# Hybrid decoder trunk: the order of the mixing stage, attention's scores one block ahead, and an output projection in one pass

## The chip, the cores and the metric

The kernel runs on one core of a Trainium2 chip. A core has a matrix engine (TensorE, in the profile PE, with its weight loads as PEld), a vector engine (DVE), a scalar engine (ACT), GpSimd (POOL), SyncE (SP, which here only issues DMAs), and 16 DMA engines. Each engine works through its own instructions in order; they wait for one another by semaphores. The metric is the device time of one execution in microseconds, lower is better.

## What is computed

Two layers over 512 tokens of width 1024, all in float32. Each layer is: half a SwiGLU feed-forward step, a mixing step, half a feed-forward step, each with a norm whose shift, scale and gate come from a condition `c`. The mixing step projects the normed tokens to 2560 columns, which feed three mechanisms side by side, joins their 1024 results and projects these back:

```python
proj = hn @ w_mix_in[l]
p_att, p_rwkv, p_conv = jnp.split(proj, [ATT_PROJ_WIDTH, ATT_PROJ_WIDTH + RWKV_PROJ_WIDTH], axis=-1)
y_att = sliding_window_sink_attention(p_att, ...)    # 8 query heads, 2 key heads, window 128: 512 columns
y_rwkv = rwkv7_time_mix(p_rwkv, ...)                 # 4 heads of a linear recurrence over time: 256 columns
y_conv = short_conv_mix(p_conv, conv_w[l])           # gated convolution of three taps: 256 columns
mixed = jnp.concatenate([y_att, y_rwkv, y_conv], axis=-1) @ w_mix_out[l]
h = h + (1.0 + gt2) * mixed
```

Attention works on blocks of 128 tokens, each against itself and the block before. The recurrence keeps a 64x64 state per head:

```python
def step(S, inp):
    r_t, w_t, k_t, v_t, kk_t, a_t = inp
    s_kk = jnp.einsum('bhvk,bhk->bhv', S, kk_t)
    S = (S * w_t[:, :, None, :] - s_kk[..., None] * (kk_t * a_t)[:, :, None, :]
         + v_t[..., None] * k_t[:, :, None, :])
    return S, jnp.einsum('bhvk,bhk->bhv', S, r_t)
```

## The kernel before

Everything is held with features on the 128 partitions and the 512 tokens along the free axis. The residual `h` is eight tiles of 128x512. Large products are done in three passes: a float32 operand is split into a rounded high part and the rest (`split`, L100: a cast on ACT, a subtraction on DVE), and high x high, high x low and low x high are summed in PSUM. `mm6` (L94) does one weight row of 128 (index `k`) for one output tile, in six matmuls of 256 columns; `mm3` is the same with three. `load_w` (L261) loads a weight tile of up to 128x8x128 on SP's queue into one of two raw buffers (`wraw`) and splits it into a pair of `wH` and `wL`, of which there are four.

The program is written in Python with generators, and a scheduler orders the instructions of each engine: what is written first has priority, and a later instruction goes ahead only where an earlier one isn't expected to be ready. In a few places (`tc.manual_schedule`, `tc.issue_after`) the written order is kept.

`mix` (L585) is the mixing step. Four routines of it run side by side:

- `products()` (L637): the twenty projection tiles (`projector`, L277, each eight `mm6` into a PSUM bank of tag `mm`), what is done with each tile, and then the output projection. The columns' order is set in `lay_out` (L1317): keys, values and four query tiles; then eight recurrent tiles (`lo`, then `k`, `r`, `v` of chain 0 and of chain 1, then `gd`); then six convolution tiles. The first three tiles of a stage use weights that were loaded in the stage before, share their sweep over `k`, and end together. `shifted` (L632) evacuates a recurrent tile with ACT and then DVE.
- `rwkv(0)` and `rwkv(1)` (L756): two chains of two heads each, in blocks of 64 tokens. A set-up (decays, two reciprocals, products of 64-row tiles), the inverse of small triangular matrices (`elim`/`inv` on DVE, with a way through DRAM there and back: `dl`, `G`, `di`, `C`), two levels of products, and at the end six steps of the state one after another (`ps_s`, L977, then DVE into `St`, L978). PSUM tags `r0` and `r1`, SBUF buffers of tags `s0` and `s1` (eight each), `u0`, `u1`.
- `attention()` (L1005): per block `scores(b)` (products `ps_sc`, then the softmax on DVE and ACT in place in `Sc`, L1037), `turned` (transposes `ps_pt` and masks), the product with the values `ps_av`. PSUM tag `x`. `Sc` has two buffers of its own, both of which one block uses.

The driving loop (L1113) lets the live routines take a step in turn. Each step of `rwkv` or `attention` yields its estimated PE time; in proportion to it `products()` is advanced, so that large products stand between the small ones. The proportion is the filling work that is left to the chains' work that is left, from the constants `RWKV_WORK, ATT_WORK, FILL_WORK` (L34); a step of `products()` (one `mm6`) counts 0.65. `attention` starts when the query tiles are there (`done` has "att"), a chain when its three tiles are there.

The output projection has eight output tiles and eight weight rows `k`: rows 0 to 3 multiply attention's results, 4 and 5 the convolution's, 6 and 7 the recurrence's. Output tiles 0 to 5 are done with rows 4, 5, 0, 1, 2, 3 once attention has ended (`done` has "ya") and are added to `h`; tiles 6 and 7 (`last`) are begun in the same way. After the loop, when both chains have ended, rows 6 and 7 are done for tiles 0 to 5 from a weight tensor of their own (`wmo2`, L1120), and these are added to `h` a second time, with the sums of squares for the next norm (`add_ss`). `close` (L382) ends tiles 6 and 7 and does the next norm beside them.

Of the kernel before, what the change touches and what calls it, by code (L numbers as in the profile page):

```python
# [30 lines left out]
PAD = 26  # L31
GAP = 448
GROUPS = ((0, 12), (12, 22))
RWKV_WORK, ATT_WORK, FILL_WORK = 29.8, 15.2, 129.6  # L34


def _columns(spec):
# [20 lines left out]
def trunk_kernel(ctx, tc, ins, out, layers=L, phases=("ffn1", "mix", "ffn2")):  # L58
# [524 lines left out]


    def mix(l, hn, ss, mp, then, ready):  # L585
        wi, wo1, wo2 = ins["wmi"], ins["wmo1"], ins["wmo2"]

        def small(name, w, bufs=2):
            return mp.tile([P, w], F32, name=name, tag=name, bufs=bufs)
# [13 lines left out]
        def EA(name):  # L603
            return mp.tile([P, T], F32, name=name, tag="ea", bufs=3)
# [27 lines left out]
        def shifted(pt, j, z):  # L632

            act(z, pt, AF.Copy, scale=got["om"][:, j : j + 1])
            stt(z[:, 1:], pt[:, : T - 1], mu[:, j : j + 1], z[:, 1:], ALU.mult, ALU.add)
            return z

        def products():
# [16 lines left out]
            ts(a0h, prm(l, "a0"), 0.5, None, ALU.mult)  # L655
            tt(gqk, prm(l, "qg"), prm(l, "kg"), ALU.mult)
            got.update(om=om, w0h=w0h, a0h=a0h)
            sq = EA("ksq")
            act(sq, pt, AF.Square)
            kt = A("kt")  # L660
# [36 lines left out]
            got.update(kt=kt, V=V, qr=qr, rq=rq)  # L697
            done.add("att")

            got["lo"] = shifted((yield from tile_()), 6, S(1, "lo"))  # L700
            act(got["lo"][:64], got["lo"][:64], AF.Tanh)
            for q in range(2):
                k_[q] = shifted((yield from tile_()), 2 + q, S(q, "k"))
                r_[q] = shifted((yield from tile_()), 0 + q, S(q, "r"))
                v_[q] = shifted((yield from tile_()), 4 + q, S(q, "v"))
                done.add(f"rwkv{q}")
            gd = shifted((yield from tile_()), 7, mp.tile([P, T], F32, name="gd", tag="gd"))
            act(gd, gd, AF.Tanh, scale=0.5)
            ts(gd, gd, 0.5, 0.5, ALU.mult, ALU.add)
            got["gd"] = gd  # L710

            yc = []
            for q in range(2):
                pt = yield from tile_()
# [9 lines left out]
                pt = yield from tile_()  # L724
                tt(cv, pt, cv, ALU.mult)
                yc.append(cv)
            xs = [pair(f"y{k}") for k in range(6)]
# [28 lines left out]
        def rwkv(q):  # L756
# [243 lines left out]
            mm(pg, got["gw"][:, cw], got["gd"], start=True, stop=True)  # L1000
            tt(y, y, pg, ALU.mult)
            yr[q] = y
            yield 0.9

        def attention():  # L1005
# [3 lines left out]

            def scores(b):  # L1010
                qs = slice(b * P, (b + 1) * P)
                both = [mp.tile([P, 4, P], F32, name="Sc", tag="Sc", bufs=2) for _ in range(2)]
                if b == 0:
                    for Sc in both:
                        nc.gpsimd.memset(Sc, -1e30)
                for i0 in (0, 2):
                    pts = [psum([P, 2, 2, P], "ps_sc") for _ in range(2)]
                    with tc.manual_schedule(engines={mybir.EngineType.PE}):
                        for i in range(2):
                            for g, pt in enumerate(pts):  # L1020
                                if b:
                                    m = mm(pt[:, i].rearrange("p a c -> p (a c)"), qr[rows[g], i0 + i, qs], kt[rows[g], (b - 1) * P : (b + 1) * P], start=True, stop=True)
                                else:
                                    m = mm(pt[:, i, 1], qr[rows[g], i0 + i, qs], kt[rows[g], qs], start=True, stop=True)
                                behind(m, free[0])
                    for Sc, pt in zip(both, pts):
                        if b:
                            nc.scalar.copy(Sc[:, i0 : i0 + 2], pt[:, :, 0])
                        free[0] = nc.vector.copy_predicated(Sc[:, i0 : i0 + 2], rep("mq", 2).bitcast(I32), pt[:, :, 1])
                    yield 1.0  # L1030
                for g, Sc in enumerate(both):
                    softmax(b, g, Sc)
                return both
# [28 lines left out]
                    both.append((t, src))  # L1062
                return both

            for b in range(NB):
                qs = slice(b * P, (b + 1) * P)
                pm = []
                for Sc in (yield from scores(b)):
                    pm.append(turned(b, Sc))
                    yield 0.4  # L1070
                po = psum([P, 4, P], "ps_av")
                for n in range(len(pm[0])):
                    for g in range(2):
                        t, src = pm[g][n]
                        m = mm(po[rows[g]].rearrange("p i q -> p (i q)"), V[:, src, rows[g]], t, start=n == 0, stop=n == len(pm[0]) - 1)
# [34 lines left out]
                    product_step()  # L1110


        xr = []  # L1113
        for q in range(2):
            x = pair("yr")
            split(*x, yr[q])
            xr.append(x)
# [11 lines left out]
        xs = got["xs"] + xr  # L1129
# [161 lines left out]
def lay_out(i):  # L1291
# [25 lines left out]
    order = [np.r_[512:768], pairs] + [rw(j) for j in (6, 2, 0, 4, 3, 1, 5, 7)]  # L1317
# [6 lines left out]
    w2 = wo[:, 512:768, : 6 * P].reshape(L, 2, P, 2, 3, P)  # L1324
    a["wmo2"] = c(w2.transpose(0, 3, 2, 4, 1, 5).reshape(L, 2, P, 6, P))
    a["lora"] = c(np.concatenate([i["rwkv_w_w2"], i["rwkv_a_w2"]], axis=1))
    a["gw2"] = c(i["rwkv_g_w2"])

# [43 lines left out]
```

## Time and profile before

| | us |
|---|---|
| median of three runs | 1913.11 |
| the three runs | 1912.78, 1913.11, 1916.35 |
| the profiled execution | 1913.21 |
| its span (first to last instruction) | 1911.2 |

A span is shorter than the time of its execution by what lies before the first and behind the last instruction, here 2.0 us. Times in the views count from the span's start. On one core the profiler shows each engine's instructions with their start and duration; who released a waiting engine is inferred from the semaphores. A row of a view of waits has the engine, the waiting tile and line, the engine, tile and line that it waited for, then the total in us, how often, and the longest. Matmuls overlap their neighbours: a matmul of 128x256 lasts 0.28 us by its row, while the next starts 0.114 us later. The two mixings lie at about 382 to 623 us and 1319 to 1561 us of the span.

### The profile page before, as it was taken

The numbers are of one execution on the slowest core, as the hardware profiler recorded it, in microseconds if no ns is written. First come the engines' busy times: TensorE is split into PE (matmuls) and PEld (weight loads), VectorE is DVE, ScalarE is ACT, GpSimd is POOL, SyncE is SP. The second block draws the span as 40 slices with busy tenths as digits, with TensorE's granted clock in tenths as the row PEclk, the third lists the DMA queues.
The fourth block names the chain that finished last, engine by engine and source line by source line (L and its number), as shares of the span: only waits on it lengthen the run. The fifth ranks groups of instructions, "written<-read, shape, count | busy, mean of one in ns | idle before, by whom it ended". The sixth has DMA issues, their size and how long they took to land. (4 is left out here: it accounts for less than half of the span.)

```text
span 1911.2 us, 37042 instructions
## 1 busy us (share of the span) xinstructions
PE 1878.8 (98%) x15504; PEld 1741.7 (91%) x15504; DVE 1399.8 (73%) x2181; ACT 837.0 (44%) x1264; POOL 130.7 (7%) x212
## 2 busy tenths in 40 slices
PE   8999999999999999999999999999999999999999
PEld 7998899897888999899899989989878899988998
DVE  7687687758976877677877776876599667864862
ACT  4443255346322554155345514544562235532551
POOL 0101100100000001110100020010000000110000
PEclk8999999999999999999999999999999999999999
DMA  7767877521312476887727678781321315774741
GB/s 300 245 168 221 271 198 229 168 70 45 79 43 81 123 198 176 278 218 199 264 62 193 171 260 242 191 278 42 93 61 49 88 34 163 209 217 130 198 140 59
DMA packets 104326, 308.46 MB, mean 161 GB/s; under 512 B 23392, under 2 KB 24416, under 8 KB 103136
## 3 DMA queue, kind: packets, MB, share of 16 engines
q1 hardware_dynamic: 75936, 203.33, 32.9%
q0 software_dynamic: 28224, 102.77, 21.7%
q8 instruction: 121, 1.98, 0.4%
q14 instruction: 45, 0.37, 0.1%
HBM read 302.66 MB, written 3.41 MB: 160 GB/s over the span
## 5 line engine op out<-in xcount | busy, mean ns | idle before, releaser
L101 ACT CAST wH<-wraw 128x1024 fp32r<-128x1024 f32 (+2 forms) x292 | 268.4, 922 | 512.6 <-PE ps_mm L91 176.8
L102 DVE TENSOR_TENSOR wL<-wraw,wH 128x1024 fp32r<-128x1024 f32 (+2 forms) x292 | 308.1, 1058 | 96.9 <-ACT wH L101 95.8
L90 PE MATMUL ps_mm<-actH,wH 128*128 128x512 f32 (+1 forms) x784 | 288.5, 368 | 0.0
L91 PE MATMUL ps_mm<-actL,wH 128*128 128x512 f32 (+1 forms) x784 | 288.0, 367 | 0.0
L92 PE MATMUL ps_mm<-actH,wL 128*128 128x512 f32 (+1 forms) x784 | 288.0, 367 | 0.0
L441 PE MATMUL ps_d<-comH,wH 128*128 128x256 f32 x816 | 226.8, 278 | 1.6 <-ACT wH L101 0.8
L443 PE MATMUL ps_d<-comH,wL 128*128 128x256 f32 x816 | 225.8, 277 | 2.3 <-DVE wL L102 2.3
L442 PE MATMUL ps_d<-comL,wH 128*128 128x256 f32 x816 | 225.5, 276 | 0.0
L98 PE MATMUL ps_mm<-hnH,wH 128*128 128x256 f32 x1040 | 214.0, 286 | 5.1 <-ACT hnH L101 2.9
L98 PE MATMUL ps_mm<-hnL,wH 128*128 128x256 f32 x1040 | 211.8, 283 | 0.0
L98 PE MATMUL ps_mm<-hnH,wL 128*128 128x256 f32 x1040 | 209.5, 281 | 0.5 <-DVE wL L102 0.5
L163 DVE SCALAR_TENSOR_TENSOR wada<-wada,crep 128x1024 f32<-128x1024 f32 x140 | 168.0, 1220 | 47.8 <-DMA wada<-in_wadaT 47.6
L102 DVE TENSOR_TENSOR wL<-sum,wH 128x1024 fp32r<-128x1024 f32 x102 | 124.8, 1224 | 74.9 <-ACT wH L101 74.7
L98 PEld LDWEIGHTS ps_mm<-hnH,wH 128*128 128x128 f32 x1040 | 159.5, 190 | 16.1 <-issue 8.2
L92 PEld LDWEIGHTS ps_mm<-actH,wL 128*128 128x128 f32 x784 | 147.8, 189 | 24.4
L90 PEld LDWEIGHTS ps_mm<-actH,wH 128*128 128x128 f32 x784 | 147.8, 189 | 24.2
L91 PEld LDWEIGHTS ps_mm<-actL,wH 128*128 128x128 f32 x784 | 147.8, 189 | 24.1
L101 ACT CAST wH<-sum 128x1024 fp32r<-128x1024 f32 x102 | 107.5, 1054 | 140.3 <-PE ps_d L442 60.1
L98 PEld LDWEIGHTS ps_mm<-hnL,wH 128*128 128x128 f32 x1040 | 160.2, 190 | 6.7 <-issue 5.7
L98 PEld LDWEIGHTS ps_mm<-hnH,wL 128*128 128x128 f32 x1040 | 160.1, 190 | 4.1 <-issue 2.9
L441 PEld LDWEIGHTS ps_d<-comH,wH 128*128 128x128 f32 x816 | 153.2, 188 | 3.9 <-ACT wH L101 1.4
L443 PEld LDWEIGHTS ps_d<-comH,wL 128*128 128x128 f32 x816 | 153.2, 188 | 2.9 <-DVE wL L102 2.9
(402 smaller groups left out, 4237.3 us busy)
## 6 DMA issues: line engine op xcount, KB each, us to landing
wada<-in_wadaT POOLq DMA_DIRECT2D x128, 512.0 KB, 4.9
wraw<-in_wmi SPq DMA_DIRECT2D x40, 512.0 KB
wraw<-in_w2p SPq DMA_DIRECT2D x36, 512.0 KB
wraw<-in_w1p SPq DMA_DIRECT2D x32, 512.0 KB
wraw<-in_w1o SPq DMA_DIRECT2D x32, 384.0 KB
wraw<-in_w2o SPq DMA_DIRECT2D x32, 384.0 KB
wraw<-in_w1i SPq DMA_DIRECT2D x20, 512.0 KB
wraw<-in_w1o SPq DMA_DIRECT2D x32, 320.0 KB
```

Source lines behind the costliest of these rows:

```text
L90: mm(acc, wH, xH, start=start, stop=False)
L91: mm(acc, wH, xL, start=False, stop=False)
L92: mm(acc, wL, xH, start=False, stop=stop)
L98: mm(acc[:, sl], w[a][:, k], x[b][:, sl], start=start and n == 0 and sl is HALVES[0], stop=stop and n == 2, skip_group_check=True)
L101: nc.scalar.copy(hi, src)
L102: nc.vector.tensor_sub(lo, src, hi.bitcast(F32))
L163: stt(w, w, 1.0, crep, ALU.mult, ALU.mult, accum_out=out_)
L441: mm(pt[:, i], wH, x[k][0], start=start and i + k == 0, stop=False, skip_group_check=True)
L442: mm(pt[:, i], wH, x[k][1], start=False, stop=False, skip_group_check=True)
L443: last = mm(pt[:, i], wL, x[k][0], start=False, stop=k == 3, skip_group_check=True)
```

## The change

- The columns of the first projection, and with them the steps of `products()`, come in another order: the eight recurrent tiles first, then keys, values and queries, then the convolution. So chain 0 starts after the fourth tile and chain 1 after the seventh, attention after the fourteenth.
- The squares of the queries (`qsq`) are held in general buffers (tag `e`) and not in those of the chains.
- `attention()` computes the scores and the softmax of block b+1 before the values of block b. `Sc` has no buffers of its own any more; it takes buffers of chain 0 (tag `s0`), four at a time instead of two.
- The output projection takes all eight rows in one pass. `products()` waits for both chains ("y0", "y1"), splits their results, and opens output tiles 0 to 3 with rows 4 to 7, in PSUM tags `r0` and `mm` in turn, with their weight pairs held. When attention has ended, rows 0 to 3 of these follow, then tiles 4 and 5 with all eight rows, then `last` as before. `wmo2`, the pass after the loop and the second addition to `h` are gone; the sums of squares are made with the one addition.
- `FILL_WORK` is 114.4 instead of 129.6.

```diff
-RWKV_WORK, ATT_WORK, FILL_WORK = 29.8, 15.2, 129.6
+RWKV_WORK, ATT_WORK, FILL_WORK = 29.8, 15.2, 114.4
...
             got.update(om=om, w0h=w0h, a0h=a0h)
+            got["lo"] = shifted(pt, 6, S(1, "lo"))
+            act(got["lo"][:64], got["lo"][:64], AF.Tanh)
+            for q in range(2):
+                k_[q] = shifted((yield from tile_()), 2 + q, S(q, "k"))
+                r_[q] = shifted((yield from tile_()), 0 + q, S(q, "r"))
+                v_[q] = shifted((yield from tile_()), 4 + q, S(q, "v"))
+                done.add(f"rwkv{q}")
+            gd = shifted((yield from tile_()), 7, mp.tile([P, T], F32, name="gd", tag="gd"))
...
+            pt = yield from tile_()
             sq = EA("ksq")
...
-                sqs.append(S(i % 2, "qsq"))
+                sqs.append(E("qsq"))
...
-            done.add("in")
+            while not {"y0", "y1"} <= done:
+                yield "stuck"
+            for k in (6, 7):
+                split(*xs[k], yr[k - 6])
+
+            def out(pt, w, ks, first=False, last=False):
+                for k in ks:
+                    mm6(pt, w, k, xs[k], first and k == ks[0], last and k == ks[-1])
+                    yield
+
+            early, late = (4, 5, 6, 7), (0, 1, 2, 3)
+            open_ = []
+            for i in range(4):
+                w, pt = load_w(wo1[l, i]), psmm(("r0", "mm"))
+                yield from out(pt, w, early, first=True)
+                open_.append((i, w, pt))
             while "ya" not in done:
                 yield "stuck"
             for k in range(4):
                 split(*xs[k], qr[:, k])
-
-            got["xs"] = xs
-            for i in range(KD - 2):
-                w = load_w(wo1[l, i, :, :6], 6)
-                pt = psmm()
-                for k in (4, 5, 0, 1, 2, 3):
-                    mm6(pt, w, k, xs[k], k == 4, k == 3)
-                    yield
-                residual(pt, i, cm, None)
+            for i, w, pt in open_:
+                yield from out(pt, w, late, last=True)
+                residual(pt, i, cm, ss)
+            for i in (4, 5):
+                w, pt = load_w(wo1[l, i]), psmm()
+                yield from out(pt, w, early + late, first=True, last=True)
+                residual(pt, i, cm, ss)
...
-                both = [mp.tile([P, 4, P], F32, name="Sc", tag="Sc", bufs=2) for _ in range(2)]
+                both = [S(0, "Sc", (P, 4, P)) for _ in range(2)]
...
+            last = None
+            for b in range(NB):
+                both = yield from scores(b)
+                if last is not None:
+                    yield from values(b - 1, last)
+                last = both
+            yield from values(NB - 1, last)
             done.add("ya")
...
-        for n in range(2):
-            w = load_w(wo2[l, n], 6)
-            for d in range(3):
-                i = 3 * n + d
-                pt = psmm(BANKS[1:3])
-                for k in range(2):
-                    mm6(pt, w, 2 * d + k, xr[k], k == 0, k == 1)
-                residual(pt, i, cm, ss)
             steps[-1](n, raws[:, n])
```

`values(b, both)` is the second half of the old loop over blocks (transposes, masks, product with the values), unchanged.

More of the change, by code (lines that the diff above doesn't have):

```diff
@@ L585, in mix @@
     def mix(l, hn, ss, mp, then, ready):
-        wi, wo1, wo2 = ins["wmi"], ins["wmo1"], ins["wmo2"]
+        wi, wo1 = ins["wmi"], ins["wmo1"]
         def small(name, w, bufs=2):
@@ L657, in products @@
             got.update(om=om, w0h=w0h, a0h=a0h)
+            got["lo"] = shifted(pt, 6, S(1, "lo"))
[6 more added lines that the diff above has]
+            gd = shifted((yield from tile_()), 7, mp.tile([P, T], F32, name="gd", tag="gd"))
+            act(gd, gd, AF.Tanh, scale=0.5)
+            ts(gd, gd, 0.5, 0.5, ALU.mult, ALU.add)
+            got["gd"] = gd
+            pt = yield from tile_()
             sq = EA("ksq")
@@ L698, in products @@
             done.add("att")
[L700 to L710, printed above, removed]
             yc = []
@@ L726, in products @@
                 yc.append(cv)
-            xs = [pair(f"y{k}") for k in range(6)]
+            xs = [pair(f"y{k}") for k in range(6)] + [pair("yr") for _ in range(2)]
+            got["xs"] = xs
             for k in (4, 5):
                 split(*xs[k], yc[k - 4])
-            done.add("in")
+            while not {"y0", "y1"} <= done:
[12 more added lines that the diff above has]
+                open_.append((i, w, pt))
             while "ya" not in done:
@@ L1002, in rwkv @@
             yr[q] = y
+            done.add(f"y{q}")
             yield 0.9
@@ L1063, in turned, with values @@
                 return both
-            for b in range(NB):
+            def values(b, both):
                 qs = slice(b * P, (b + 1) * P)
                 pm = []
-                for Sc in (yield from scores(b)):
+                for Sc in both:
                     pm.append(turned(b, Sc))
@@ L1110, in mix @@
                     product_step()
[L1113 to L1117, printed above, removed]
         steps = then()
@@ L1120, in mix @@
         for n in range(2):
[L1121 to L1127 removed]
             steps[-1](n, raws[:, n])
[L1129 removed]
+        xs = got["xs"]
         seq = lambda w, ks: [(w, k, xs[k]) for k in ks]
@@ L1316, in lay_out @@
     cv = lambda j: np.r_[1792 + j * P : 1792 + (j + 1) * P]
-    order = [np.r_[512:768], pairs] + [rw(j) for j in (6, 2, 0, 4, 3, 1, 5, 7)]
+    order = [rw(j) for j in (6, 2, 0, 4, 3, 1, 5, 7)] + [np.r_[512:768], pairs]
     order += [cv(j) for j in (2, 4, 0, 3, 5, 1)]
```

2 lines of the change are left out of this document (removed).

## The prediction

> **What bounds the kernel now.** First the page's head, for the engine that has no room:
>
> ```profile
> span 1911.2 us, 37042 instructions
> ...
> PE 1878.8 (98%) x15504; PEld 1741.7 (91%) x15504; DVE 1399.8 (73%) x2181; ACT 837.0 (44%) x1264; POOL 130.7 (7%) x212
> ```
>
> TensorE (PE) is the bound, and the change issues the same products, so only PE's idle time, and matmuls that run slower than they could, can be won. The view by stretches of time tells where these are. It has per row: the stretch, its length, then busy time and count for PE, weight loads, DVE, ACT, POOL, then granted clock, DMA share and GB/s. Row one is a feed-forward stretch for comparison, rows two and three are the two mixings, the last two are stages of the first mixing.
>
> ```profile
> 50.00:100.00 50.00, 50.00 (x438) 50.00 (x438) 35.16 (x50) 19.89 (x25) 6.42 (x12) 1.00 0.74 244
> 382.00:623.00 241.00, 233.67 (x2585) 205.16 (x2584) 177.93 (x370) 101.34 (x208) 1.84 (x6) 1.00 0.23 63
> 1319.00:1561.00 242.00, 234.07 (x2578) 205.51 (x2578) 177.85 (x370) 101.23 (x208) 1.86 (x6) 0.99 0.22 63
> 455.00:545.00 90.00, 86.44 (x1082) 72.38 (x1081) 82.39 (x203) 37.50 (x85) 0.85 (x4) 1.00 0.21 54
> ...
> 585.00:623.00 38.00, 36.20 (x316) 33.55 (x315) 24.71 (x36) 11.98 (x18) 0.00 (x0) 1.00 0.17 51
> ```
>
> A 128x256 matmul takes 50/438 = 0.114 us, so one `mm6` (six of them, one weight row of one tile) 0.685 us and a projection tile of eight 5.5 us. In the mixings PE idles 241 - 233.7 = 7.3 us and 242 - 234.1 = 7.9 us: 15.2 us of 1911 is what a better order can reach directly. Half of it lies in the stage 455:545, where DVE is busy 82.4 of 90 us (attention and both recurrent set-ups at once), and 1.8 us at the end. The view of PE's waits names them, in the first mixing (ten rows) and the second (the last row, its longest; its others are within 0.2 us of these, and the wait on `St` is absent):
>
> ```profile
> PE ps_s L977 <- ACT y L972: 1.4, 1, 1.4
> PE ps_bo L611 <- DVE bonus L800: 0.9, 2, 0.5
> PE ps_ks L611 <- ACT ksq L659: 0.8, 1, 0.8
> PE ps_pt L1057 <- DVE Sc L1050: 0.7, 2, 0.4
> PE ps_sc L1022 <- DVE Sc L1029: 0.7, 1, 0.7
> PE ps_o L964 <- DVE N L954: 0.6, 1, 0.6
> PE ps_c L824 <- DVE B L828: 0.5, 1, 0.5
> PE ps_pt L1057 <- DVE den L1048: 0.5, 1, 0.5
> PE ps_s L977 <- DVE St L978: 0.4, 1, 0.4
> PE ps_x L916 <- DVE T L907: 0.4, 1, 0.4
> ...
> PE ps_s L977 <- ACT y L972: 2.2, 1, 2.2
> ```
>
> **The change, part by part.** (1) The end of the recurrent chain. The timeline shows what stands behind its longest wait:
>
> ```profile
> 583.81 4.86 SPq L267 DMA_DIRECT2D wraw<-in_wmo  x2
> ...
> 587.09 1.22 DVE L102 TENSOR_TENSOR wL<-wraw,wH 128x1024 fp32r<-128x1024 f32 x1 [3.31 <-ACT wH L101]
> ...
> 589.11 0.33 PE L977 MATMUL ps_s<-St,GT 64*64 64x64 f32 x4 [1.36 <-ACT y L972]
> ```
>
> DVE works in order: a weight split that waits for its load (3.31 us) stands ahead of the chain's own DVE operation, and PE, also in order, waits at `ps_s`. After the change the second recurrent chain starts when seven projection tiles are done, not thirteen; counting the yields and the credit in the driving loop by hand, its last step falls beside the last of the twenty projection tiles, with all output tiles still to come. I take these waits as gone: 1.4 + 0.4 in the first mixing, 2.2 in the second. The second costs more than its length:
>
> ```profile
> 1525.00:1530.00 5.00, 3.55 (x21) 3.14 (x21) 3.13 (x6) 1.44 (x3) 0.00 (x0) 0.68 0.43 99
> ```
>
> The granted clock is 0.68 here, so 5 x 0.32 = 1.6 us of full-speed work is missing, of which between 1.1 (the share of the time in which PE was busy) and 1.6 is lost; I take 1.2. Sum -(1.8 + 2.2 + 1.2) = **-5.2 us**, from 0 (the same happens elsewhere) to -5.6. The Trainium skill (TensorE: Matmul & The Clock Gate, "What's actually happening") says that the clock halves after at least one idle window of about 3.4 us; the trace disagrees, as the clock falls here after an idle time of 2.2 us. By the page the 1.2 us would not be there and the sum would be -4.0 us.
>
> (2) Attention's scores one block ahead, in the recurrent buffers of chain 0 (eight of tag `s0`) in place of two of its own. `scores(b)` no longer waits for the transposes of b-1, and other work lies between a softmax and its transposes: the rows of `ps_pt` and `ps_sc` go, 0.7 + 0.5 + 0.7 = 1.9 us in the first mixing and 1.8 in the second, **-3.7 us**; ends 0 and -3.7.
>
> (3) The first tile is now a recurrent one. At the start of the stage three tiles end together and the fourth needs a PSUM bank of them:
>
> ```profile
> 398.82 1.22 DVE L102 TENSOR_TENSOR wL<-wraw,wH 128x1024 fp32r<-128x1024 f32 x1 [4.05 <-ACT wH L101]
> 399.18 0.58 ACT L661 COPY kt<-ps_mm 128x512 f32<-128x512 f32 x1
> ...
> 399.34 1.12 PE L611 MATMUL ps_ks<-ksq,con 128*128 128x512 f32 x2 [0.84 <-ACT ksq L659]
> ...
> 399.90 0.68 PE L98 MATMUL ps_mm<-hnH,wH 128*128 128x256 f32 x1
> ```
>
> Now two ACT operations free the bank, while `ps_ks` fills 0.56 us of the hole (399.34 to 399.90). `shifted` needs ACT and then DVE, where a 1.22 us split may stand ahead: bank free 0.25 to 0.95 us later, and the 0.56 us of `ps_ks` falls due elsewhere, less the 0.1 us or so that it costs to change from one kind of matmul to the other. +0.7 to +1.4 us per mixing; middle, two mixings: **+2.0 us**.
>
> (4) A new wait. Four output tiles are opened with rows 4 to 7 and stay open until attention is done; they hold all four weight pairs and both `mm` banks, so no other output tile can start. Behind PE's wait stand their 16 late `mm6`, and everything after. Counting yields, the work beside the last softmax is nine `mm6` (6.2 us), two blocks' transposes (2.0) and value products (4.2), 12.4 us. The chain beside it is read from block 0 (PE's timeline, last scores and value product):
>
> ```profile
> 424.38 0.71 PE L1024 MATMUL ps_sc<-kt,qr 64*128 64x128 f32 x8
> ...
> 437.15 1.08 PE L1075 MATMUL ps_av<-pmc,V 128*64 128x512 f32 x4
> ```
>
> From the end of the scores, 425.1, to the value product 12.1 us; with a product of two parts (2 x 1.08) and two ACT copies of some 0.6 (as `kt` above) before the first late `mm6`, 15.4 us. Uncovered 3.0 us per mixing at the one end. At the other nothing: if the recurrent chain lags the hand-count, rows 6 and 7 wait, attention runs ahead and they become its cover. I take the middle, 1.5 each, **+3.0 us**.
>
> (5) What costs nothing. The output's second pass goes: with it six residual additions per mixing on DVE; its twelve `mm6` stand now among the others; PE was fed through that stage but for the waits in (1), so none of it was on the path. Weights: six loads of 384 KB, two of 512 and two of 384 become eight of 512 KB, the same 4096 KB. The recurrent chains' small loads and stores move ahead of the weight loads of tile 6 and on in SP's queue; four split pairs and two raw buffers (some four tiles, 22 us of PE) cover a stop. POOL clears two score tiles later, with nothing behind it there. The other waits (`ps_bo`, `ps_o`, `ps_c`, `ps_x`, 2.4 us a mixing) may move, not go: DVE's work is the same.
>
> Sum -5.2 - 3.7 + 2.0 + 3.0 = -3.9 us. The profiled execution took 1913.21 us (span 1911.2 and 2.0 around it), 0.1 over the median of 1913.11: **1909.3, so 1909.2 us.**
>
> **Rivals.** *Tail uncovered* (speaks for it: the counted 12.4 against 15.4 us, and ACT and DVE also split weights there): 3.0 us in each mixing, and the clock falls as in (1), 1.2 each: -5.2 - 3.7 + 2.0 + 8.4 = +1.5, 1914.6 us; 20%. By the Trainium skill's 3.4 us (the page and section named in (1)) the clock would hold and this would be 1912.2 us.
> *Slower: splits come late.* Both set-ups now start in the first third and are earlier in DVE's order than the splits of tile 4 and on:
>
> ```profile
> L102 DVE TENSOR_TENSOR wL<-wraw,wH 128x1024 fp32r<-128x1024 f32 x21 | 25.4, 1215 | 18.7 <-ACT wH L101 18.7
> ...
> L791 DVE RECIPROCAL iP<-P 128x512 f32<-128x512 f32 x2 | 6.7, 3344 | 0.0
> L792 DVE RECIPROCAL rn<-rn 128x512 f32<-128x512 f32 x2 | 6.7, 3335 | 0.0
> ```
>
> Two reciprocals are 6.7 us in one block. If they stand ahead of a split whose tile PE is about to need, half of it, 3.3 us, shows, once per set-up, four times: +13.3, 1922.5 us. It decides from 1 us each (the gain is eaten). Against it: the same saturation in 455:545 cost PE 3.6 of 90 us and no row of the waits names a split; four pairs lie ahead. 14%.
> *The look-ahead does nothing*, since chain 0 still holds its eight buffers when block 1's scores are due: the 3.7 us stay, 1913.0 us; against it, chain 0's last step precedes attention's first in the count; 8%.
> *More is won*: DVE's load is spread, the waits on it in (5) go too (2 x 2.4 us) and the tail is covered (no 3.0): 1909.3 - 4.8 - 3.0 = 1901.5 us; 20%. The Trainium skill (Perfetto Trace Analysis, "Identifying the Most-Contended Engine") judges PE's headroom by weight loads, not matmuls; here that is 205 of 241 us, 36 us of room in a mixing where the matmul row leaves 7; I don't take it, as small matmuls of 64 rows are in both.
>
> **How the numbers follow.** The forecast has 38% (1905 to 1913). Range: from 1900 (more is won, less 1.5) to 1918 (tail uncovered, with the start's upper end and one late split), which leaves out the 14% and a few per cent below. A measurement of this kernel can tell about 0.2%, 3.8 us, from no change. Faster: of the forecast 24 of 38, and "more is won", 44%. Same: the other 14, of "tail uncovered" 15 of 20, and the look-ahead's 8, 37%. Slower: 5 and 14, 19%.
>
> **What would show it.** Right: no wait of `ps_s` on `y` over 0.5 us and no clock under 1.00 in either mixing; `ps_pt` and `ps_sc` out of the waits; the first L98 matmul of the fourth tile 0.2 to 1 us later after the third tile; a first late `mm6` (reading `y0`) that waits 0 to 3 us. Wrong: L98 matmuls that wait for `wL` or `wH` in the first third (splits late), or a clock drop where the late rows begin (tail).

## The result, and the profile after

| | median us | runs, range | against before |
|---|---|---|---|
| before | 1914.48 | 4, 1912.78 to 1916.35 | |
| after | 1940.26 | 4, 1935.17 to 1941.79 | 1.0135 [1.0115, 1.0155] |

The kernel became 1.35% slower (95% interval 1.15 to 1.55%). The forecast was 1909.2 us, its range ended at 1918: the time lies outside, on the other side. The profiled execution of after took 1935.17 us, the fastest of the four, so its trace shows some 5 us less of the loss than the median does.

The head of the page of after:

```profile
span 1933.3 us, 37019 instructions
...
PE 1882.0 (97%) x15504; PEld 1748.1 (90%) x15504; DVE 1394.2 (72%) x2165; ACT 849.0 (44%) x1268; POOL 131.1 (7%) x212
```

PE has the same 15504 matmuls. DVE has 16 operations and 5.6 us less. ACT has 12.0 us more, most of it eight more loads of a function table (`ACT_TABLE_LOAD`, 1.28 us each, 26 instead of 18). These loads alone aren't the loss: with another `FILL_WORK`, below, there are 30 of them in a kernel that is as fast as before. The span grew by 22.1 us. The views by stretches say where: a mixing is taken here from its first product (`ps_ss`) to the next stage, so that the stretches of the two kernels hold the same work. Before, the two mixings:

```profile
372.70:622.60 249.90, 242.57 (x2661) 214.06 (x2660) 183.83 (x383) 105.37 (x217) 1.84 (x6) 1.00 0.22 61
1309.10:1560.70 251.60, 243.68 (x2660) 215.11 (x2659) 183.82 (x383) 105.29 (x216) 1.86 (x6) 0.99 0.21 60
```

After, the two mixings, then three short stretches of the first:

```profile
372.70:632.60 259.90, 242.22 (x2662) 216.03 (x2660) 181.11 (x375) 109.85 (x218) 1.91 (x6) 0.98 0.20 59
1318.50:1582.20 263.70, 246.10 (x2662) 218.98 (x2660) 181.06 (x375) 109.92 (x218) 1.91 (x6) 0.96 0.20 58
401.70:405.10 3.40, 3.40 (x18) 3.40 (x17) 1.56 (x3) 3.24 (x4) 0.00 (x0) 0.50 0.60 180
500.60:504.00 3.40, 3.04 (x43) 2.92 (x43) 2.21 (x6) 0.00 (x0) 0.00 (x0) 0.51 0.30 117
579.20:582.60 3.40, 3.40 (x11) 1.26 (x7) 2.75 (x4) 2.09 (x4) 0.00 (x0) 0.51 0.40 102
```

The mixings are 10.0 and 12.1 us longer: the whole 22.1 us. Length less PE's busy time is its idle time: 7.3 and 7.9 us before, 17.7 and 17.6 after, so some 10 us more each. The other quantity is the granted clock. In the three short stretches it is 0.50, against one such stretch (3.4 us, in the second mixing) in both mixings of before: 10.2 us at half clock in the first mixing and, read in the same way, 20.5 in the second, where two stretches are twice as long. Work done at half clock takes about twice the time (in the median, successive matmuls of 128x256 start 0.213 us apart there and 0.114 elsewhere), so about half of that time is lost. For the first mixing: +10.4 idle, +5 clock, and so about -5 of something that became shorter; for the second +9.7, +8.5 and -6. That gain comes last in this document.

PE's waits, from the first mixing of after; the last row is from the second, which else has the same rows (its wait at `ps_av` is 3.3, its longest 1.8):

```profile
PE ps_av L1091 <- DVE pmp L1077: 6.0, 2, 4.5
PE ps_x L931 <- DVE T L922: 2.9, 1, 2.9
PE ps_mm L98 <- DVE lo L635: 2.3, 1, 2.3
PE ps_bo L611 <- DVE bonus L815: 2.3, 2, 1.5
PE ps_vN L882 <- DVE K L843: 1.4, 1, 1.4
PE ps_mm L98 <- ACT y0H L101: 1.3, 1, 1.3
PE ps_c L839 <- DVE B L843: 0.6, 2, 0.3
PE ps_pt L1073 <- DVE Sc L1066: 0.3, 1, 0.3
...
PE ps_mm L98 <- ACT wH L101: 2.2, 1, 2.2
```

`ps_s` is gone from the list and `ps_pt` all but gone, as forecast. New are `ps_av`, `ps_vN` and the three L98 rows, and `ps_x` and `ps_bo` have grown: mostly waits for DVE, now bare at other places. The timeline shows the longest (PE and DVE, in order of start):

```profile
400.76 0.51 PE L98 MATMUL ps_mm<-hnH,wH 128*128 128x256 f32 x2 [2.27 <-DVE lo L635]
...
569.83 3.34 DVE L1007 RECIPROCAL gnrs<-gnrs 128x512 f32<-128x512 f32 x1
...
571.06 0.40 PE L98 MATMUL ps_mm<-hnH,wL 128*128 128x256 f32 x2
...
573.64 0.40 PE L98 MATMUL ps_mm<-y4H,wL 128*128 128x256 f32 x2
...
577.74 0.68 DVE L1077 TENSOR_TENSOR pmp<-ps_pt,con 128x512 f32<-128x512 f32 x1
...
578.57 1.45 PE L1091 MATMUL ps_av<-pmc,V 128*64 128x512 f32 x4 [4.53 <-DVE pmp L1077]
...
580.67 1.28 DVE L102 TENSOR_TENSOR yrL<-y,yrH 128x512 fp32r<-128x512 f32 x2
...
599.87 1.08 PE L1091 MATMUL ps_av<-pmc,V 128*64 128x512 f32 x4 [1.47 <-DVE pmp L1077]
...
603.14 0.95 PE L98 MATMUL ps_mm<-y0H,wH 128*128 128x256 f32 x6 [1.32 <-ACT y0H L101]
```

The last matmul of the projection (reading `hn`) is at 571.06. What is left then for PE beside attention are output rows 4 to 7. Row 4 of three of the four open tiles is done by 574.0; rows 5 to 7 need the last convolution result and both chains' results, whose splits come on DVE only at 580.07 to 582, behind the second chain's group norm (a reciprocal of 3.34 us and three operations), one block's softmax and another block's masks (`pmc`, `pmp`). PE stands for 4.53 us. Attention still has two value products to come, the last at 600, where PE waits again: 0.30 + 1.47 + 1.32 us.

### The profile page after: what moved, and what is told of

It reads as the page before. It is cut to its first block, busy times and chain, and to the rows that moved or that the text cites. A ratio compares the mean times of both kernels' runs of the same rounds, so it can differ in the third digit from the quotient of the medians.

```text
span 1933.3 us, 37019 instructions
## 1 busy us (share of the span) xinstructions
PE 1882.0 (97%) x15504; PEld 1748.1 (90%) x15504; DVE 1394.2 (72%) x2165; ACT 849.0 (44%) x1268; POOL 131.1 (7%) x212
## 3 DMA queue, kind: packets, MB, share of 16 engines
HBM read 302.66 MB, written 3.41 MB: 158 GB/s over the span
## 5 line engine op out<-in xcount | busy, mean ns | idle before, releaser
L98 PE MATMUL ps_mm<-hnH,wH 128*128 128x256 f32 x1040 | 217.7, 291 | 9.7 <-DVE lo L635 4.5
L98 PE MATMUL ps_mm<-hnL,wH 128*128 128x256 f32 x1040 | 213.6, 285 | 0.0
L98 PE MATMUL ps_mm<-hnH,wL 128*128 128x256 f32 x1040 | 212.5, 285 | 0.5 <-DVE wL L102 0.5
L98 PEld LDWEIGHTS ps_mm<-hnH,wH 128*128 128x128 f32 x1040 | 161.9, 192 | 22.0 <-issue 7.5
L91 PEld LDWEIGHTS ps_mm<-actL,wH 128*128 128x128 f32 x784 | 147.8, 189 | 24.2
L90 PEld LDWEIGHTS ps_mm<-actH,wH 128*128 128x128 f32 x784 | 147.8, 189 | 24.2
L98 PEld LDWEIGHTS ps_mm<-hnL,wH 128*128 128x128 f32 x1040 | 162.2, 192 | 6.7 <-issue 6.1
L98 PEld LDWEIGHTS ps_mm<-hnH,wL 128*128 128x128 f32 x1040 | 162.1, 192 | 4.0 <-issue 2.5
```

The lines of the kernel that those rows point to most:

```text
L90: mm(acc, wH, xH, start=start, stop=False)
L91: mm(acc, wH, xL, start=False, stop=False)
L98: mm(acc[:, sl], w[a][:, k], x[b][:, sl], start=start and n == 0 and sl is HALVES[0], stop=stop and n == 2, skip_group_check=True)
```

## The experiments

The theory at first: the loss is made of holes with causes of their own (the bank at the start, the open output tiles at the end), each with a clock drop behind it. The rivals: the order itself leaves too little filling work beside the recurrence and attention; or the look-ahead is what costs.

**One part at a time.** First, the fourth tile gets a bank of another tag (line in `projector`):

```diff
-            pt = psmm(tags)
+            pt = psmm(("r0",) if n == 3 and tags == ("mm",) else tags)
```

> The changed kernel, with the fourth projection tile of each mixing in a free PSUM bank (tag r0), so that it need not wait until the first tile is evacuated. Theory (each wait of PE over about 1.5 us costs itself and then up to 1.7 us by a halved clock): the 2.3 us wait at the start of each mixing and the clock drop behind it go, 2 x (2.3 + 1.2) = 7 us less than the changed kernel's 1940, 1933 us. Rival (the wait only moves to the next tile, or the clock drops elsewhere instead): 1938 to 1941 us.

1937.89 us (1935.57 to 1941.26), 1.0129 [1.0114, 1.0145]: no gain. The L98 wait on `lo` is gone, and its stall stands 20 us later, at `ps_bo`. Its waits, and in its windows the clock there:

```profile
PE ps_av L1091 <- DVE pmp L1077: 6.0, 2, 4.5
PE ps_bo L611 <- DVE bonus L815: 3.5, 2, 2.8
```
```profile
420.40:427.40 7.00, 4.18 (x24) 2.98 (x25) 6.71 (x13) 3.28 (x5) 0.42 (x2) 0.76 0.07 21
```

The longest wait for `bonus` rose from 1.5 to 2.8 us, with a clock of 0.76 around it. Filling one hole moved the stall to the next product that DVE was late for.

Second, after without the look-ahead (scores and values of a block in turn):

```diff
-            last = None
             for b in range(NB):
-                both = yield from scores(b)
-                if last is not None:
-                    yield from values(b - 1, last)
-                last = both
-            yield from values(NB - 1, last)
+                yield from values(b, (yield from scores(b)))
```

> The changed kernel without the look-ahead: scores and values of one block after the other, in the same buffers. Theory (the order costs, the look-ahead gains some 4 us of attention's waits): 1942 to 1948 us. Rival (the look-ahead puts the value product of block 1 beside the end of the second recurrent chain, and so makes the wait of 4.5 us of ps_av on DVE with the clock drop behind it): that wait goes, 1928 to 1936 us.

1967.95 us (1961.7 to 1969.57), 1.0275 [1.0255, 1.0295]; in this order the look-ahead is a gain of 27.7 us. Its first mixing and its longest wait:

```profile
373.20:649.50 276.30, 250.13 (x2660) 219.76 (x2659) 182.00 (x375) 109.95 (x218) 1.92 (x6) 0.93 0.19 55
```
```profile
PE ps_pt L1073 <- DVE Sc L1066: 10.0, 4, 6.3
```

Third, before with nothing but the recurrent tiles ahead (two blocks of `products()` and the columns swapped, `qsq` in the general buffers, `FILL_WORK` still 129.6):

```diff
-    order = [np.r_[512:768], pairs] + [rw(j) for j in (6, 2, 0, 4, 3, 1, 5, 7)]
+    order = [rw(j) for j in (6, 2, 0, 4, 3, 1, 5, 7)] + [np.r_[512:768], pairs]
```

> The kernel before with the new order of the projection tiles alone (recurrent first, squares of the queries in general buffers); attention without look-ahead, output in two passes, FILL_WORK 129.6. Theory (the order is what costs, by the wait at the start and by those of the recurrent set-ups ps_bo, ps_vN, ps_x): 1925 to 1935 us. Rival (the tail of the one-pass output behind attention and its meeting with the second chain's end cost): 1910 to 1918 us.

1976.7 us (1973.37 to 1980.88), 1.0332 [1.0315, 1.0349]; its longest wait:

```profile
PE ps_pt L1058 <- DVE Sc L1051: 19.4, 4, 10.2
```

Attention runs last now, and each softmax is bare: 19.4 us of `ps_pt` in one mixing. This is where the inquiry turned. The constant 129.6 is filling work to be spread over the chains' work, but only 155 counted steps of projection can stand before attention's end here, 155 x 0.65 = 101; so all of it is used before the last blocks. The run thus mixes the order with a constant that doesn't fit it.

Fourth, the mirror image: before's order with one pass of output, in which four open tiles wait for rows 6 and 7 (`yr`) instead:

```diff
+            early, late = (4, 5, 0, 1, 2, 3), (6, 7)
...
+            while not {"y0", "y1"} <= done:
+                yield "stuck"
+            for k in (6, 7):
+                split(*xs[k], yr[k - 6])
```

> The kernel before in its old order, with the output in one pass in mirror image: tiles 0 to 3 are opened with attention's and the convolution's six rows and stay open until the recurrent chains are done, then rows 6 and 7, then tiles 4 and 5 with all rows. If one pass is harmless by itself: 1910 to 1917 us, the longest wait of ps_s on y still there. If open tiles that hold the weight pairs starve PE: over 1920 us, with waits before the late rows.

1923.99 us (1922.36 to 1926.14), 1.0056 [1.0041, 1.0071]. One row tells it:

```profile
PE ps_mm L98 <- ACT yrH L101: 6.3, 1, 6.3
```

The pass after the loop had been the cover of the recurrence's end. Fifth, before with the look-ahead alone (score tiles of odd blocks in `s0`, the squares of the queries in the general buffers):

```diff
+                both = [S(0, "Sc", (P, 4, P)) if b % 2 else mp.tile([P, 4, P], F32, name="Sc", tag="Sc", bufs=2) for _ in range(2)]
```

> The kernel before with the look-ahead alone: old order of the tiles, output in two passes, score tiles of even blocks in their own two buffers and of odd blocks in those of chain 0, squares of the queries in general buffers. Theory (the look-ahead takes attention's waits of PE, 3.7 us, and nothing else changes): 1909 to 1911 us. Rival (score tiles in chain 0's buffers hold back chain 0's set-up, or attention's waits only move): 1912 to 1920 us.

1929.52 us (1927.85 to 1933.02), 1.0086 [1.0064, 1.0108]. In the old order the look-ahead, which is worth 27.7 us in the new one, costs 16: the value product of block 1 now waits at `ps_av` for masks that DVE makes in between the softmax of block 2 (`es`), and `ps_sc` waits more than before (0.7).

```profile
PE ps_av L1075 <- DVE es L1043: 2.8, 1, 2.8
PE ps_sc L1022 <- DVE Sc L1029: 2.0, 3, 1.3
```

So no part has a price of its own; each depends on what is written beside it. The last three runs kept the constant 129.6, and it was not fitted to any of them, so how much of their loss is the part and how much the constant isn't shown. The new theory: `FILL_WORK` is what is wrong. 114.4 is more than the (155 + 16 early rows) x 0.65 = 111 that can stand before attention's end by the hand-count, so nothing is left there.

**The constant.** One number is changed in after. In the last of these five runs it is the order with the look-ahead and before's output (two passes), with 100.8, which is its 155 steps:

```diff
-RWKV_WORK, ATT_WORK, FILL_WORK = 29.8, 15.2, 114.4
+RWKV_WORK, ATT_WORK, FILL_WORK = 29.8, 15.2, 98.0    # 106.0, 110.0, 112.0 in the others
```

> The changed kernel with FILL_WORK 98 in place of 114.4, so that in the written order more of the early output rows come behind attention's last block. Theory (what is lost in the last third of a mixing, the waits of ps_av and of the first late row with the clock drops behind them, is a chain without work beside it): these waits shrink, 1925 to 1933 us. Rival (the scheduler moves ready work forward anyhow, so the constant changes little): 1936 to 1942 us.

> The changed kernel with FILL_WORK 106, between 98 (1918.8 us) and 114.4 (1940). Theory (171 written steps of 0.65, 111 in all, can stand before attention's end; a constant over 111 uses them up too early, under it some stay for the end): near the good end, 1918 to 1925 us. Rival (the loss grows evenly with the constant): 1927 to 1933 us.

> The changed kernel with FILL_WORK 110, just under the 111 that the steps before attention's end add up to. If the loss is a step at 111: 1909 to 1914 us, as with 106. If it grows as fewer early output rows are left for attention's last block (by the hand-count all 16 are left with 98 and 106, fewer from there on, none with 114.4): between 106 and 114.4, 1918 to 1930 us, with a wait of the first late row of 1 to 2 us.

> The changed kernel with FILL_WORK 112, just over 111. If the loss is a step at 111: over 1930 us. If it grows as the early rows are used up: 1920 to 1933 us, 3 to 8 us over the run with 110.

> The new order with the look-ahead, but the output in two passes as before, and FILL_WORK 100.8, which counts only the steps that can stand before attention's end (155 of 0.65). Theory (the one-pass output gives the end of attention work to stand beside, rows 4 to 7 of four tiles, 11 us a mixing; without it this is missing): slower than the changed kernel, 1950 to 1965 us. Rival (the one pass itself costs, as it did in the old order, some 10 us): 1925 to 1933 us.

Each ratio goes by the runs of before that were made beside it (medians 1912.85 to 1914.48). The half-clock times are multiples of 3.41 us, read from the granted clock; they and the idle times are those of the one profiled execution.

| `FILL_WORK` | median us (runs) | against before | PE idle, two mixings | half clock, two mixings |
|---|---|---|---|---|
| before, 129.6 | 1914.48 (4) | | 7.3, 7.9 | 0, 3.4 |
| after, 98 | 1918.76 (7) | 1.0036 [1.0023, 1.005] | 13.0, 12.0 | 6.8, 6.8 |
| after, 106 | 1910.94 (10) | 0.9983 [0.9972, 0.9994] | 10.7, 9.8 | 10.2, 0 |
| after, 110 | 1915.23 (10) | 1.0013 [1.0002, 1.0024] | 11.7, 12.5 | 6.8, 0 |
| after, 112 | 1926.08 (4) | 1.0073 [1.0056, 1.009] | 14.2, 14.1 | 17.1, 13.7 |
| after, 114.4 | 1940.26 (4) | 1.0135 [1.0115, 1.0155] | 17.7, 17.6 | 10.2, 20.5 |
| new order, look-ahead, two passes, 100.8 | 1918.79 (7) | 1.003 [1.0019, 1.0041] | 12.1, 10.9 | 6.8, 3.4 |

One constant moves the changed kernel by 29.3 us, more than the whole loss. 98 and 106 came out 6 and 7 us under the ranges of their theories, 110 between its two, 112 in its range but 10.9 us over 110 and not 3 to 8, and the two passes far under both of theirs. It isn't a step at 111 but a steep rise from 110 on: the constant sets a proportion, so the last blocks lose their cover by degrees. From 110 to 114.4 the idle time rises by 35.3 - 24.2 = 11.1 us and the time at half clock by 30.7 - 6.8 = 23.9, of which half is 11.9: together 23.0, as the two profiled spans differ (1910.3 and 1933.3). The timeline of after with 106, at the same place:

```profile
575.78 0.48 PE L98 MATMUL ps_mm<-hnH,wL 128*128 128x256 f32 x2
...
579.42 1.08 PE L1091 MATMUL ps_av<-pmc,V 128*64 128x512 f32 x4 [1.00 <-DVE es L1059]
...
588.14 1.03 PE L1091 MATMUL ps_av<-pmp,V 128*64 128x512 f32 x4
...
594.74 0.40 PE L98 MATMUL ps_mm<-y0H,wH 128*128 128x256 f32 x2
```

Projection lasts to 576 instead of 571.5. The 4.53 us wait is 1.0. Attention's last product is at 588 instead of 601, and between it and the first late row stand early rows that were left over, so that this row waits for nothing. What is left of waits, and the two mixings:

```profile
PE ps_x L931 <- DVE T L922: 2.8, 1, 2.8
PE ps_mm L98 <- DVE lo L635: 2.3, 1, 2.3
PE ps_bo L611 <- DVE bonus L815: 2.0, 2, 1.5
PE ps_av L1091 <- DVE es L1059: 1.0, 1, 1.0
```
```profile
372.60:624.50 251.90, 241.20 (x2662) 216.88 (x2660) 180.76 (x375) 111.23 (x220) 1.91 (x6) 0.98 0.21 60
1313.30:1559.90 246.60, 236.76 (x2662) 212.67 (x2660) 180.67 (x375) 111.42 (x220) 1.91 (x6) 1.00 0.21 62
```

The second mixing, with no clock drop, is 5.0 us shorter than before's; the first, with 10.2 us at half clock, 2.0 longer. This is the best version of the study, faster than before by 0.17% (0.06 to 0.28%), which is less than the 0.2% that the prediction took as what can be told. Before's own constant was not swept, so it isn't shown that before with another constant would be slower than this.

The run with two passes and 100.8 equals after with 98 within 0.1 us. So the one pass isn't needed to come close to before; what it is worth by itself isn't shown, since two passes were run with this constant alone, and one pass is 7.8 us faster with 106 than with 98.

Does the look-ahead's size depend on the constant too?

> The changed kernel with FILL_WORK 106 and without the look-ahead. Theory (in the new order attention comes last and is a chain of four blocks, which the look-ahead shortens, whatever the constant): slower than with the look-ahead (1911) by 10 us or more, with waits of ps_pt. Rival (once some output rows are left for the end, they cover the chain in either form): within 5 us, 1909 to 1916 us.

1934.1 us (1932.02 to 1936.22), 1.0108 [1.0093, 1.0123]: without the look-ahead 106 gives 23.2 us more than with it, and the `ps_pt` waits are back (6.4 us in the first mixing, the longest 3.0). Order, look-ahead and constant belong together (each with the one-pass output): the first two without the third give 1940, the first and the third 1934, all three 1911. Without the look-ahead only 106 and 114.4 were run, so its size at a constant fitted to that form isn't known.

**The remaining holes.** With 98, by the hand-count, more filling is left for the end than is needed, and the waits stand earlier: `ps_x` for `T`, 4.7 us in the first mixing, with the clock at half behind it. Its timeline (SP's queue, DVE, PE) shows the way through DRAM:

```profile
493.46 4.40 SPq L874 DMA_DIRECT2D C<-di  x8
499.40 0.69 DVE L922 TENSOR_TENSOR T<-C,con 128x512 f32<-128x512 f32 x1 [5.32 <-DMA C<-di]
500.14 1.28 PE L931 MATMUL ps_x<-T,B 64*64 64x64 f32 x20 [4.70 <-DVE T L922]
```

Eight issues of 8 KB take 4.4 us one after another on SP. So three more runs: the bank at the start again, the loads of `C` from two queues, and both, all with 98.

```diff
-                    nc.sync.dma_start(
+                    (nc.gpsimd if m % 2 else nc.sync).dma_start(
```

> The changed kernel with FILL_WORK 98 and the fourth projection tile in bank r0. Theory (the start's wait of 2.3 us a mixing moves to ps_bo, as with 114.4): 1916 to 1920 us, no change. Rival (with the rest of the stage filled it is won, 2 x 2.3 us and a clock drop): 1911 to 1915 us.

> The changed kernel with FILL_WORK 98 and every second of the eight small loads of C issued from GpSimd instead of SyncE. Theory (the longest wait left, ps_x on T, 4.7 and 3.7 us, is the issue of eight loads one after the other on one queue, some 4.4 us, which the scheduler reckons shorter): the wait falls by some 2 us in each mixing, 1912 to 1916 us. Rival (the way through DRAM is long whatever the queue, or the wait moves): 1917 to 1921 us.

> The changed kernel with FILL_WORK 98, the fourth tile in bank r0 and the loads of C on two queues. If both waits are won: 1906 to 1911 us, faster than the kernel before. If they only move: 1915 to 1920 us.

1919.76 (1917.15 to 1922.52), 1.0032 [1.0021, 1.0042]; 1927.98 (1924.01 to 1931.88), 1.0072 [1.0051, 1.0094]; 1926.16 (1924.86 to 1927.92), 1.0061 [1.0042, 1.008]. The bank again only moves the wait to `ps_bo` (2.8 us). Two queues cost 9 us over 98 alone, and the wait that they were meant for is there still:

```profile
PE ps_x L931 <- DVE T L922: 5.0, 1, 5.0
```

`T` starts 8.3 us after the store of `di` is issued (488.53 to 496.80) where it took 9.3 with one queue (490.07 to 499.40), so two queues win 1.0 us there, not the 2 or more that halving the issues would give. The two profiled executions are 13.2 us apart (that of two queues is the slowest of its four). The mixings are 3.9 and 5.6 us longer, with 13.7 us at half clock in each instead of 6.8. Another 3.7 us lie between the mixings, where the edit has no instruction (345.9 us, from 629.8 to 975.7, against 342.2 with 98 alone; 345.9 again in the run with both edits). There PE's waits for weight splits add up to 4.5 us instead of 1.6; why the splits come later is open.

**The clock by itself.** After, with nine 128x512 products of constants into an unused bank in the hole at 398 to 401:

```diff
+            if tags == ("mm",):
+                pw = psum([P, T], "ps_warm", "r0")
+                for _ in range(9):
+                    mm(pw.rearrange("p (a b) -> p a b", b=P), ones_r, ones_r.unsqueeze(1).to_broadcast([P, 4, P]), start=True, stop=True)
```

> The changed kernel with nine extra matmuls of 128x512 on constants at the start of each mixing, where PE waits 2.3 us for the first tile's evacuation; they add no work to the path if they end before it does. Theory (the clock falls because PE is idle there, and costs up to 1.7 us): no clock drop within 5 us behind the start, and the fourth tile's 48 matmuls take 5.5 us, not over 6.5. Rival (the clock falls for another reason): the drop at that place stays.

One time, 1937.16 us, between the runs of after. The hole is full and the clock stays up, and 20 us later it falls instead:

```profile
398.50:403.50 5.00, 4.79 (x36) 4.21 (x35) 4.03 (x5) 4.97 (x8) 0.00 (x0) 1.00 0.35 105
420.40:427.40 7.00, 5.38 (x48) 4.03 (x46) 6.39 (x11) 3.93 (x5) 0.42 (x2) 0.76 0.09 21
```

So the drop at 401 follows from PE's idleness there, but a drop taken away at one place is not 1.7 us won: a wait of 1.47 us at `ps_bo`, which had passed without one in the profiled execution of after, got it here. Both waits lie whole in one window of the grid that the last section describes, with 1.62 us of idle time in it each; that is in the narrow band where some windows are followed by a drop and some are not, and what decided it is open.

## Why the prediction was wrong

**(1) The end of the chain, -5.2.** Right for the waits: no `ps_s` row above 0.2 us in after. Its 1.2 us for the clock was not won, since drops came elsewhere.

**(2) The look-ahead, -3.7, ends 0 and -3.7.** The rows went as forecast (`ps_pt` 0.3 left, `ps_sc` none), but the term had no such size. It was worth 27.7 us against the new order without it, 23.2 with 106, and cost 16 in the old order with before's constant. Counting the rows of before prices a part in before's order; in an order in which attention runs last the part's price is another.

**(3) The start, +2.0 (0.7 to 1.4 a mixing).** The wait is there, 2.27 us instead of 0.84, and the fourth tile's first L98 matmul is at 400.76 instead of 399.90: 0.86 us, between the 0.25 and 0.95 of the estimate. What the term left out is the drop behind it. The Trainium skill (TensorE: Matmul & The Clock Gate, "What's actually happening") has the clock at half after an idle window of about 3.4 us; here 2.27 us brought it down. Step (1) had shown the same of before (2.2 us) and priced it at one place only.

**(4) The new wait at attention's end, 1.5, ends 0 and 3.0.** Measured: 0.30 + 1.47 + 1.32 = 3.1 us, the uncovered end of the two. The hand-count of nine `mm6` beside the last softmax was right too: nine stand there in the timeline of after, from 587.4 to 597.5. But it looked at the last softmax alone and did not ask what stands beside the blocks ahead of it. There the 4.5 us arose (1.8 in the second mixing, with 2.2 more for a weight split).

**(5) "What costs nothing", and the constant: the step that failed.** The prediction wrote that the other waits "may move, not go". They moved and grew: `ps_x` 0.4 to 2.9, `ps_bo` 0.9 to 2.3, `ps_vN` from nothing to 1.4. And of `FILL_WORK`, which the diff lowers from 129.6 to 114.4, it priced nothing; the constant served only to count what falls where. At 114.4 all the filling work that may stand before attention's end is used before it, and the waits of DVE's chains lie bare. The runs put 29.3 us on that constant alone (114.4 against 106). In the two profiled executions, whose mixings differ by 25.1 us, 14.7 of it is idle time and 20.5 / 2 = 10.2 the clock. What the constant takes away in the first mixing is most of `ps_av` (6.0 to 1.0), the wait on `y0H` and half of `ps_vN`. The waits on `lo` and of `ps_bo` stay (2.3 and 2.0 us with 106, much the same with the other constants) and belong to the new order; `ps_x` is 2.8 us with 106, 0.7 with 110 and 4.7 with 98.

**The rivals.** "Tail uncovered" (1914.6) had the right kind of mechanism, attention without work beside it, but at the last softmax alone and far too small: it had one wait and one drop per mixing, 8.4 us in all, where the first mixing's trace has seven waits of 1.3 us and more and three drops, none of them where the late rows begin. (The time given for it without drops, 1912.2, still counts the 1.2 us of (1) as won; without them the sum is 1913.4.) "Splits come late" is not the cause: the first mixing of after has no L98 wait on a split of weights, the second one, 2.2 us. "The look-ahead does nothing" and "more is won" fall for after as it is. Of the five signs that were to show the forecast right, four came, `ps_pt` but for 0.3 us; only the clock didn't hold, and neither sign of its being wrong was there. The signs looked at the waits that had been priced, and the loss lay in others. With 106 the time is 1910.9, near the forecast; that doesn't confirm its terms, since waits of 8.1 us in that first mixing stand where the forecast had others, and a gain that it didn't have (below) pays for them.

## What to carry to other kernels

When a change moves a chain of short dependent steps to the end of a stage, count the independent work that is left at each step of it, not only at its last; the constant that spreads this work is a term of the sum, and should be swept again with the new order before the order is judged. A wait that a profile shows is a price in that order only: taking it away mostly moves it to the next product whose input is late. Where the matmul clock falls behind idle time as it does here, price each wait of more than some 1.7 us with its length and, as likely as not, half of the slow stretch behind it.

## What was not expected of the hardware

**The clock falls by a grid in time.** All clock drops of one execution begin on a grid of 3.413 us. In after: 401.7, 500.6 (29 steps later), 579.2 (23 more), 1347.2 (225 more), and so on; the same holds in each of the 17 traces, each with an offset of its own. So the trace can be cut into the grid's windows, and PE's idle time before matmuls summed in each. Between 60 and 1900 us of these 17 traces, of the windows that began at full clock, all 59 with over 1.8 us of idle time were followed by a window at half clock, none of the 8922 with under 1.6 us, and 13 of the 20 between. The same wait can thus cost a drop or not, by where the grid's edge falls. After with 106, the windows around its two waits of 2.27 us on `lo`, 398.4 to 400.6 and 1339.1 to 1341.4:

```profile
398.49:401.90 3.41, 1.26 (x10) 1.26 (x11) 3.20 (x5) 3.39 (x6) 0.00 (x0) 1.00 0.28 62
401.90:405.31 3.41, 3.41 (x18) 3.41 (x17) 1.57 (x2) 2.92 (x4) 0.00 (x0) 0.50 0.58 204
1337.17:1340.58 3.41, 1.97 (x18) 1.77 (x16) 1.12 (x1) 2.20 (x4) 0.00 (x0) 1.00 0.00 0
1340.58:1343.99 3.41, 2.59 (x22) 2.59 (x23) 3.22 (x5) 3.38 (x6) 0.00 (x0) 1.00 0.57 159
```

In the first mixing one window holds 2.15 us of it, and the next runs at 0.50. In the second the edge at 1340.58 cuts the wait into 1.44 and 0.82 us, and the clock stays. By this a wait of 2.27 us is spared where both its parts stay under 1.7, for 1.1 of the edge's 3.4 us of places: one time in three, if the offset is by chance. The offset is another in each execution; that may be why filling or moving one hole gave so little, and why the runs of one kernel spread by 6 us, but no run set the offset. The Trainium skill (TensorE: Matmul & The Clock Gate, "What's actually happening") has a free-running window of about 3.4 us, and the grid here agrees. It has the clock at half after an idle window; by these traces the window needs to be idle for only about half of its length.

**Cheaper matmuls.** PE's busy time in the second mixing with 106 is 236.76 us, in before's first 242.57, both with a clock of 1.00 and the same matmuls: 5.8 us less. Summed from the start of each matmul to that of the next, without the waits, `ps_c` takes 4.2 us instead of 5.6, `ps_w` 3.8 instead of 4.8, `ps_q` 1.3 instead of 2.0, `ps_s` 2.5 instead of 3.0, and the large `ps_mm` 170.9 instead of 172.2. It is most of what the order wins, and no term of the prediction had it.

Changes from one kind of matmul to another are a part of it. There are 164 places in before's first mixing where two successive matmuls differ in size or in the rows and columns of the array that they use, and 130 in the second mixing with 106. What a change costs can be read from the starts: in before, a matmul of 128x256 is followed by its like after 0.123 us in the mean and by one of 64x64 after 0.221; one of 64x64 is followed by its like after 0.024 us and by one of 128x256 after 0.148. Summed over all changes, what they take over the mean between two of the same kind falls from 11.9 to 7.8 us: by this estimate 4.1 of the 5.8. After with 114.4 has 142 and 144 changes and 9.6 and 9.9 us, some of it at half clock. The prediction had the price of a change, 0.1 us, in its term (3), but did not count the changes. No run altered their number alone, and the rest of the gain is open.
